# A hybrid DeltaNet layer on one Trainium2 core: delta values turned by VectorE over DRAM, the queries' sums of squares by VectorE and a small transfer

## The chip, the core and the metric

The kernel runs on one core of a Trainium2 chip. The core has TensorE (PE, with its weight loads PEld), VectorE (DVE), ScalarE (ACT), GpSimd (POOL) and SyncE (SP), each with its own queue of instructions that it takes in order; transfers are issued by an engine and then run on the core's 16 DMA engines. The metric is the device time of one execution in microseconds, as the median of several. The profile is of one execution.

## The reference

Two layers of a decoder trunk over 256 tokens with 1024 channels, batch 1, all in f32. A layer is a SwiGLU half step, a layer norm, three token mixers side by side on one combined input projection (gated DeltaNet, sliding-window attention, attention to a memory), gates, a projection of each mixer and of their gated sum, a layer norm, another SwiGLU half step and a layer norm. The change is in the DeltaNet mixer, of 4 heads with 128 channels:

```python
qkv = silu(causal_depthwise_conv(concat([q, k, v]), conv_w))
q = q * rsqrt(sum(q * q, -1) + 1e-6)            # per token and head
k = k * rsqrt(sum(k * k, -1) + 1e-6)
o = gated_delta_rule(q, k, v, g, beta)          # chunks, a triangular inverse each
o = o * rsqrt(mean(o * o, -1) + 1e-6) * norm_w
o = o * silu(z)
```

The kernel does not scale q and k themselves. It carries the keys' norms `kn` into the values (`vin` = v times kn, by token), and the queries' sums of squares into the epsilon of the last norm (`qeps` = 128e-6 times (sum of q squared + 1e-6)).

## The kernel before

Tokens come in two blocks of 128. All weights pass through one stream of units of 128 x 1024 f32. SP loads a unit into `raw` (4 buffers); ACT casts it to `whi`, DVE subtracts to `wlo` (`split`, L125; 5 buffers each), and PE multiplies it in three passes (every matmul is recorded at L134, the helper). A unit is released for the next when PE has used it. The stream runs ahead of PE by these buffers, and ACT and DVE take its casts and splits between all other work, in one fixed order for each engine that a scheduler made. PE's own order in the mixers is as written (`pinned`).

`conv` projects k, q and v channel by channel with tokens along the free axis (`kT`, `qT`, `vT`). What is needed with tokens on partitions is turned by PE: `tok` puts four 128x128 transposes (L137) into one PSUM bank. `tok_k` (during q's projection) and `tok_q` (during v's) take the sums of squares from there with a square on ACT and a reduction on DVE; `tok_v` (during the projection of the memory queries) multiplies the turned values by `kn` into `vin`.

Behind this, gates and branch projections are woven with small steps: `weave` runs a step's functions after the n-th yield of the projection, about 12 matmuls each. `inverses` (L783) sends the diagonal blocks over DRAM to POOL, which inverts them; `begin_inverse` (L902) hands them to DVE; seven calls of `double` join blocks on PE, with copies on ACT, DVE (L852, L853) and POOL (L878). Then `rec_v0` reads `vin` of block 0 on PE, `rec_s1` builds the state, `rec_r1` forms R1 on DVE (L945) from `vin` of block 1, and `rec_v1` reads R1 on PE. `finish` (L917) reads `qeps`. `branch(1)` holds its four units until its last group of matmuls; DVE multiplies each group by its gate (L998), and POOL adds it to the sum (L1000).

The FFN already turns its hidden activations without PE: `out` (L347) transposes 32x32 blocks on DVE (L356), writes them with four DMAs to DRAM (L362) and reads them back with one (L363), both issued by POOL.

Of the kernel before, what the change touches and what calls it, by code (L numbers as in the profile page):

```python
# [14 lines left out]
ALU = mybir.AluOpType  # L15
# [23 lines left out]
def tile_trunk(ctx, tc, x, xT, mem, memT_, wst, lnp, memln, cvw, rows, cst, out):  # L39
# [22 lines left out]
    def T(pool, shape, tag, dt=F32, bufs=None):  # L62
        pool = pn if pool is pu and tag in NEAR else pool
        kw = {} if bufs is None else {"bufs": bufs}
        return pool.tile(shape, dt, tag=tag, name=nm(tag), **kw)
# [79 lines left out]
    def weave(work, steps):  # L145

        for n, _ in enumerate(work, 1):
            for f in steps.get(n, ()):
                f()
# [374 lines left out]
    def mixers(l, hT, mkT, mv_, post):  # L524
# [35 lines left out]
        ktok = T(pu, [P, 4, P], "u9")  # L560
        vin = T(pu, [P, 2, 4, P], "u2")
        rk2 = T(pu, [P, 2, 4], "rk2")
# [24 lines left out]

        def tok_v():
            for tb in range(2):
                ps = tok(vT, tb)  # L590
                nc.vector.tensor_tensor(vin[:, tb], ps, kn[:, tb, :].unsqueeze(2).to_broadcast([P, 4, P]), op=ALU.mult)

        def tok_q():
            for tb in range(2):
                sumsq(tok(qT, tb), ssq[:, 1, tb, :])
            nc.vector.tensor_scalar(qeps, ssq[:, 1], RMS_EPS, RMS_EPS * P, ALU.add, ALU.mult)

        weave(conv(1, kT), {})
        weave(conv(0, qT), {3: [tok_k]})
        weave(conv(2, vT), {3: [tok_q]})  # L600

# [166 lines left out]
        def w_values(tb):  # L768
            if not oS:
                oS.extend(T(pu, [P, 4, S], tag, F32R) for tag in ("u6", "u7"))  # L770
            ts = slice(tb * P, (tb + 1) * P)
            pso = at()
            for kb in range(tb + 1):
                for kv in range(2):
                    hs = slice(kv * 64, kv * 64 + 64)
                    matmul(pso[hs, :], swv[:, kb, hs], wpT[tb][kb][:, kv].rearrange("p h q -> p (h q)"), start=kb == 0, stop=kb == tb)
            split(oS[0][:, :, ts], oS[1][:, :, ts], pso.rearrange("p (h k) -> p h k", h=4))

# [44 lines left out]

        weave(halves(xt, use_xq), {3: [tok_v]})
        (b,) = projB(xt, 1, 8)
# [12 lines left out]
        def doubling(c):  # L838
# [13 lines left out]
            nc.vector.tensor_tensor(Y32[:, c], Y32[:, c], ps, op=ALU.subtract)  # L852
            nc.vector.transpose(W[:, 512 + c * P:512 + c * P + P], W[:, 768 + c * P:768 + c * P + P])  # L853
            yield
# [22 lines left out]
            for q in qd:  # L877
                nc.gpsimd.tensor_copy(Yc[q, :, q], Y32[q, c])  # L878
            yield
# [56 lines left out]
        def rec_v0():  # L936
            nc.scalar.copy(V0, heads(lambda h: (Y[:, 0, h, :], vin[:, 0, h, :])))

# [3 lines left out]
        def rec_r1():  # L942
            ps = heads(lambda h: (kT[:, h, c1], S1[:, h, :]))
            for h in range(4):
                nc.vector.scalar_tensor_tensor(R1[:, h, :], ps[:, h, :], neg1[:, h:h + 1], vin[:, 1, h, :], op0=ALU.mult, op1=ALU.add)  # L945

# [38 lines left out]
        def branch(n, o):  # L985
# [4 lines left out]
            for tb in range(2):  # L990
                ts = slice(tb * P, (tb + 1) * P)
                for j in range(2):
# [4 lines left out]
                    dst = gt[tb] if n else mg[tb]  # L997
                    nc.vector.scalar_tensor_tensor(dst[:, js], gt[tb][:, js], 1.0, ps, op0=ALU.add, op1=ALU.mult)  # L998
                    if n:
# [17 lines left out]
            2: [lambda: w_scores(1, 1)],  # L1017
            3: [double],
            5: [double, lambda: w_turn(1, 0)],
            6: [double, lambda: w_turn(1, 1)],  # L1020
            7: [double, lambda: w_values(1)],
            8: [double]})
        weave(branch(1, oS), {
            1: [double],
            2: [rec_v0],
            3: [rec_s1],
            4: [rec_r1]})
# [176 lines left out]
```

## Time and profile before

| what | before |
|---|---|
| median of 3 runs | 1274.08 us (1273.45 to 1274.12) |
| profiled execution, span from the first to the last instruction | 1272.1 us |
| PE busy | 1260.6 us, 99% |
| DVE / ACT / POOL busy | 864.1 / 661.4 / 207.2 us |
| mean granted TensorE clock | 0.998 |

The profiled execution's own time is its span of 1272.1 us; the median of the runs is 1.98 us more, for what lies around the first and the last instruction. In a timeline a row gives start and duration in us, then engine, line of the kernel, operation, the tile written and the tiles read, and in brackets how long the engine was idle just before and on whom it waited. In the groups of instructions the figures behind the bar are busy us, mean ns of one, and idle us before. The chain of waits follows the work that ended last back from the end.

### The profile page before, as it was taken

Reading aid. Unit: us, or ns where it says so; the run is one execution under the profiler, and the core shown is the slowest. Engines: PE = TensorE matmul, PEld = TensorE weight load, DVE = VectorE, ACT = ScalarE, POOL = GpSimd, SP = SyncE. Lnnn points to the kernel's source line nnn. Section 1 sums busy time; section 2 is a strip of 40 time slices with the busy share of each in tenths; the row PEclk is TensorE's granted clock in tenths of the full one; section 3 lists DMA queues with packets and bytes.
Section 4 is the critical chain, followed back from the end, with each engine's and each line's share of the span. In section 5 each row is a group of like instructions: output and inputs, shape, how many; then the busy total and the mean of one; then the engine's idle time right before and its main releaser. Section 6 shows DMA issues by size and latency. Waiting matters only on the chain.

```text
span 1272.1 us, 18768 instructions
## 1 busy us (share of the span) xinstructions
PE 1260.6 (99%) x6948; PEld 1073.3 (84%) x6948; DVE 864.1 (68%) x1274; ACT 661.4 (52%) x982; POOL 207.2 (16%) x365
## 2 busy tenths in 40 slices
PE   9999999999999999999999999999999999999997
PEld 6888889999778888888888888899987788888886
DVE  6678576886647776665766665759867387766565
ACT  6456444655664544454454554456556554454441
POOL 1232000002311102221012220000023101122100
PEclk9999999999999999999999999999999999999999
DMA  8988765655534748877668877566463356577762
GB/s 294 317 271 289 248 208 159 211 171 129 172 117 144 241 141 259 241 241 220 217 210 244 256 252 219 177 185 213 150 167 134 100 189 225 174 246 244 241 220 82
DMA packets 77643, 261.40 MB, mean 205 GB/s; under 512 B 11920, under 2 KB 13328, under 8 KB 77552
## 3 DMA queue, kind: packets, MB, share of 16 engines
q1 hardware_dynamic: 66320, 232.40, 56.0%
q0 software_dynamic: 11088, 27.68, 8.1%
q8 instruction: 54, 0.88, 0.3%
q14 instruction: 37, 0.30, 0.1%
q10 hardware_dynamic: 144, 0.13, 0.0%
HBM read 246.40 MB, written 13.76 MB: 205 GB/s over the span
## 4 chain that ended last, share of the span: by engine, by line
PE 89%; DMA 3%; POOL 3%; DVE 2%; issue 2%; ACT 0%; SPq 0%; DVEq 0%; POOLq 0%; ACTq 0%
PE acc L134 80%; PE at L134 3%; PE sm L134 2%; DMA w<-dr 2%; PE sm L137 2%; DVE wlo L125 1%; DMA raw<-in_wst_dram 1%; POOL t L808 1%; POOL t L807 1%; PE acc L332 1%; PE acc L333 1%; POOL l L798 1%; PE acc L335 1%; DMA dr<-t 1%; ACT whi L125 0%
## 5 line engine op out<-in xcount | busy, mean ns | idle before, releaser
L125 DVE TENSOR_TENSOR wlo<-raw,whi 128x1024 fp32r<-128x1024 f32 (+2 forms) x405 | 487.0, 1210 | 279.7 <-ACT whi L125 277.5
L125 ACT CAST whi<-raw 128x1024 fp32r<-128x1024 f32 (+2 forms) x405 | 413.7, 1029 | 400.6 <-PE acc L134 316.2
L134 PE MATMUL acc<-whi,hT 128*128 128x512 f32 (+1 forms) x1824 | 562.2, 386 | 0.5 <-ACT whi L125 0.5
L134 PEld LDWEIGHTS acc<-whi,hT 128*128 128x128 f32 x1824 | 340.0, 188 | 69.8 <-ACT whi L125 2.3
L134 PE MATMUL acc<-wlo,hT 128*128 128x512 f32 (+1 forms) x912 | 350.2, 384 | 0.0
L134 PE MATMUL acc<-whi,u 128*128 128x512 f32 x812 | 259.5, 392 | 0.0
L134 PEld LDWEIGHTS acc<-wlo,hT 128*128 128x128 f32 x912 | 171.3, 188 | 33.1 <-DVE wlo L125 1.0
L134 PEld LDWEIGHTS acc<-whi,u 128*128 128x128 f32 x812 | 152.3, 188 | 32.1 <-DVE u L125 0.5
L134 PE MATMUL acc<-wlo,u 128*128 128x512 f32 x406 | 158.2, 390 | 0.0
L362 POOL DMA_DIRECT2D tr<-t x176 | 96.3, 554 | 311.6 <-DVE t L356 303.5
L134 PE MATMUL acc<-hT,whi 128*128 128x256 f32 x672 | 122.2, 284 | 0.0
L134 PEld LDWEIGHTS acc<-hT,whi 128*128 128x128 f32 x672 | 104.6, 192 | 0.0
L134 PE MATMUL acc<-hT,wlo 128*128 128x256 f32 x336 | 95.0, 283 | 0.0
L134 PEld LDWEIGHTS acc<-wlo,u 128*128 128x128 f32 x406 | 76.3, 188 | 15.4
L134 PEld LDWEIGHTS acc<-hT,wlo 128*128 128x128 f32 x336 | 64.3, 191 | 0.0
L363 POOL DMA_DIRECT2D pt<-tr x44 | 25.0, 569 | 192.5 <-DMA tr<-t 138.4
L353 ACT ACTIVATE t<-acc 128x256 f32<-128x256 f32 x88 | 33.5, 381 | 36.9 <-PE acc L134 36.9
L134 PE MATMUL acc<-u,u 128*128 128x512 f32 x186 | 46.4, 394 | 0.0
L354 DVE TENSOR_TENSOR t<-t,acc 128x256 f32<-128x256 f32 x88 | 36.6, 417 | 8.1 <-ACT t L353 4.1
L1000 POOL TENSOR_TENSOR u<-u,gt 128x512 f32<-128x512 f32 x16 | 20.7, 1294 | 125.0 <-DVE gt L998 125.0
L134 PEld LDWEIGHTS acc<-u,u 128*128 128x128 f32 x186 | 34.6, 188 | 7.5
L125 DVE TENSOR_TENSOR u<-pt,u 128x512 fp32r<-128x512 f32 x44 | 28.9, 657 | 9.4 <-ACT u L125 9.4
(236 smaller groups left out, 1165.0 us busy)
## 6 DMA issues: line engine op xcount, KB each, us to landing
raw<-in_wst_dram SPq DMA_DIRECT2D x409, 512.0 KB, 4.4
tr<-t POOLq DMA_DIRECT2D x176, 64.0 KB, 3.8
pt<-tr POOLq DMA_DIRECT2D x44, 256.0 KB, 5.0
raw<-in_wst_dram SPq DMA_DIRECT2D x16, 324.0 KB, 3.0
gB<-in_lnp_dram SPq DMA_DIRECT2D x6, 512.0 KB, 5.8
bB<-in_lnp_dram SPq DMA_DIRECT2D x6, 512.0 KB, 6.2
w<-dr POOLq DMA_DIRECT2D x4, 512.0 KB, 12.0
t<-in_xT_dram SPq DMA_DIRECT2D x4, 256.0 KB, 5.2
```

The lines of the kernel that those rows point to most:

```text
L125: return nc.scalar.copy(hi, src).ins, nc.vector.tensor_tensor(lo, src, hi.bitcast(F32), op=ALU.subtract).ins
L134: return pe(nc.tensor.matmul(*a, **k))
L137: return pe(nc.tensor.transpose(*a))
L332: nc.tensor.matmul(ps, hT[0][:, k, ts], hi[:, c], start=k == 0, stop=False)
L333: nc.tensor.matmul(ps, hT[0][:, k, ts], lo[:, c], start=False, stop=False)
L335: nc.tensor.matmul(ps, hT[1][:, k, ts], hi[:, c], start=False, stop=k == KD - 1)
L353: act = nc.scalar.activation(t[:, :, tb, :], g, AF.Silu).ins
L354: ins = nc.vector.tensor_tensor(t[:, :, tb, :], t[:, :, tb, :], u, op=ALU.mult).ins
L362: nc.gpsimd.dma_start(d[:, :, q].rearrange("b c x -> c b x"), z[32 * q:32 * q + 32].rearrange("c (b x) -> c b x", b=4))
L363: back = nc.gpsimd.dma_start(y, d.rearrange("b c q x -> (b c) (q x)")).ins
L798: nc.gpsimd.tensor_tensor(L32[q, c], AK[c][q, :, 0, q], cs[q, C_LV:C_LV + 32].unsqueeze(1).to_broadcast([32, 4, 32]), op=ALU.mult)
L1000: nc.gpsimd.tensor_tensor(mg[tb][:, js], mg[tb][:, js], gt[tb][:, js], op=ALU.add)
```

## The change

q's and v's transposes leave PE. `tok_q` and `tok_v` are gone; in their place stand five functions, in the doubling's steps (`gates(1)` and `branch(1)`).

- `leave_v` (step 3 of `gates(1)`): for each token block DVE turns 32x32 blocks of `vT` into a tile `z`, and POOL writes it with four DMAs to DRAM (`tv`, 64 KB each).
- `back_v` (step 5): for each block one DMA on POOL reads it back into `vin`, whose layout is now channel group, head, channel (256 KB each).
- `land_v` (step 7): DVE scales `vin` in place by `kn`, once a block.
- `leave_q` (step 8): for each block ACT squares `qT`, DVE turns the squares and reduces groups of 32 columns to `part`; one DMA on POOL writes all of `part` (128x32, 16 KB) to DRAM, and four read it back (4 KB each, in pieces of 32 bytes) with tokens on partitions.
- `land_q` (step 3 of `branch(1)`): DVE adds the four parts and forms `qeps`.

`held` puts each of these behind the instruction last noted in `late` on the same engine; this orders the queues and adds no wait of its own. `rec_v0` and `rec_r1` read `vin` in its new layout.

```diff
-        def tok_v():
-            for tb in range(2):
-                ps = tok(vT, tb)
-                nc.vector.tensor_tensor(vin[:, tb], ps, kn[:, tb, :].unsqueeze(2).to_broadcast([P, 4, P]), op=ALU.mult)
-
-        def tok_q():
+        def squares(src, tb):
+            return src[:, :, tb * P:(tb + 1) * P].rearrange("p h (q j) -> p q h j", q=4)
+
+        def leave_v():
             for tb in range(2):
-                sumsq(tok(qT, tb), ssq[:, 1, tb, :])
+                z = T(p2, [P, 512], "t2", bufs=4)
+                nc.vector.transpose(z, squares(vT, tb))
+                d = T(pd, [4, 32, 4, P], "tv")
+                for a in range(4):
+                    nc.gpsimd.dma_start(d[:, :, a].rearrange("t j x -> j t x"), z[32 * a:32 * a + 32].rearrange("j (t x) -> j t x", t=4))
+                turned_v.append(d)
+
+        def back_v():
+            for tb in range(2):
+                nc.gpsimd.dma_start(vin[:, tb].rearrange("p a h i -> p (a h i)"), turned_v[tb].rearrange("t j a x -> (t j) (a x)"))
+
+        def land_v():
+            for tb in range(2):
+                late["dve"] = nc.vector.tensor_tensor(vin[:, tb], vin[:, tb], kn[:, tb, :].unsqueeze(1).unsqueeze(3).to_broadcast([P, 4, 4, 32]), op=ALU.mult).ins
+
+        def leave_q():
+            part = T(p2, [P, 4, 8], "oqs")
+            for tb in range(2):
+                sq = T(p2, [P, 512], "t2", bufs=4)
+                nc.scalar.activation(sq.rearrange("p (q h j) -> p q h j", q=4, h=4), squares(qT, tb), AF.Square)
+                z = T(p2, [P, 512], "t2", bufs=4)
+                nc.vector.transpose(z, sq)
+                nc.vector.tensor_reduce(part[:, :, tb * 4:tb * 4 + 4], z.rearrange("p (q h i) -> p q h i", q=4, h=4), axis=AX.X, op=ALU.add)
+            d = T(pd, [4, 32, 4, 8], "tq")
+            nc.gpsimd.dma_start(d.rearrange("a j t x -> (a j) t x"), part)
+            sums_q.append(T(p2, [P, 4, 8], "oqr"))
+            for t in range(4):
+                nc.gpsimd.dma_start(sums_q[0][32 * t:32 * t + 32], d[:, :, t].rearrange("a j x -> j a x"))
+
+        def land_q():
+            nc.vector.tensor_reduce(ssq[:, 1].rearrange("p t h -> p (t h)"), sums_q[0].rearrange("p a x -> p x a"), axis=AX.X, op=ALU.add)
             nc.vector.tensor_scalar(qeps, ssq[:, 1], RMS_EPS, RMS_EPS * P, ALU.add, ALU.mult)
...
-        weave(conv(2, vT), {3: [tok_q]})
+        weave(conv(2, vT), {})
...
-        weave(halves(xt, use_xq), {3: [tok_v]})
+        weave(halves(xt, use_xq), {})
...
-            3: [double],
-            5: [double, lambda: w_turn(1, 0)],
+            3: [double, lambda: held(leave_v)],
+            5: [double, lambda: w_turn(1, 0), lambda: held(back_v)],
             6: [double, lambda: w_turn(1, 1)],
-            7: [double, lambda: w_values(1)],
-            8: [double]})
+            7: [double, lambda: w_values(1), lambda: held(land_v)],
+            8: [double, lambda: held(leave_q)]})
         weave(branch(1, oS), {
             1: [double],
             2: [rec_v0],
-            3: [rec_s1],
+            3: [rec_s1, lambda: held(land_q)],
             4: [rec_r1]})
```

The order of the queues at three places, all in layer 0 (layer 1 has the same). The lines of the changed kernel are higher by 38 from here on.

First DVE behind v's convolution, where `g` is formed, on which `decay`'s matmul waits (`spp` are the steps of a softplus, `u` a split of the memory queries, `swk` the window's keys). Before:

```order
L633 SCALAR_TENSOR_TENSOR spp_2575<-spp_2575,spz_456_2573 128x8
L125 TENSOR_TENSOR u_466_2597<-acc_2666,u_465_2596 128x512
L634 SCALAR_TENSOR_TENSOR spp_2575<-spp_2575,spz_2569 128x8
L635 TENSOR_SCALAR spp_2575<-spp_2575 128x8
L636 SCALAR_TENSOR_TENSOR spp_2575<-spt_2564,spp_2575 128x8
L638 TENSOR_TENSOR g_2586<-spp_2575,nea 128x8
L125 TENSOR_TENSOR wlo_2974<-raw_2972,whi_2973 128x1024
L125 TENSOR_TENSOR swk_100<-acc_2741,swk_99 64x256 x2
```

And now:

```order
L671 SCALAR_TENSOR_TENSOR spp_2558<-spp_2558,spz_452_2556 128x8 x3
L672 SCALAR_TENSOR_TENSOR spp_2558<-spp_2558,spz_2552 128x8
L673 TENSOR_SCALAR spp_2558<-spp_2558 128x8
L674 SCALAR_TENSOR_TENSOR spp_2558<-spt_2547,spp_2558 128x8
L125 TENSOR_TENSOR wlo_2945<-raw_2943,whi_2944 128x1024
L676 TENSOR_TENSOR g_2569<-spp_2558,nea 128x8
L125 TENSOR_TENSOR swk_100<-acc_2712,swk_99 64x256 x2
```

`g` now stands behind the split that it stood ahead of.

Then POOL from the end of the inverse on (`w` are the doubling's tiles, `u` with `tv` is `vin`, `u` with `gt` the merged sum). Before:

```order
L809 TENSOR_TENSOR w_470_2601<-t_535_3053,cs 128x256
L878 COPY w_471_2602<-w_470_2601 32x4x32 x8
L1000 TENSOR_TENSOR u_592_3349<-u_592_3349,gt_3450 128x512 x2
L1000 TENSOR_TENSOR u_593_3350<-u_593_3350,gt_3451 128x512 x2
L1000 TENSOR_TENSOR u_592_3349<-u_592_3349,gt_3944 128x512 x2
```

And now:

```order
L847 TENSOR_TENSOR w_466_2584<-t_529_3024,cs 128x256
L916 COPY w_467_2585<-w_466_2584 32x4x32 x8
L605 DMA tv_3591<-t_627_3589 32x4x128 x4
L605 DMA tv_3598<-t_629_3596 32x4x128 x4
L610 DMA u_390_2079<-tv_3591 128x512
L610 DMA u_390_2079<-tv_3598 128x512
L627 DMA tq_3827<-oqs_3816 128x32
L1038 TENSOR_TENSOR u_586_3320<-u_586_3320,gt_3421 128x512
L630 DMA oqr_3829<-tq_3827 32x4x8 x4
L1038 TENSOR_TENSOR u_586_3320<-u_586_3320,gt_3421 128x512
L1038 TENSOR_TENSOR u_587_3321<-u_587_3321,gt_3422 128x512 x2
```

The four ways back of the sums stand behind the first product of the branch, and the other three products behind them.

Last DVE from the split of the window's output (`u` of `at`) to R1 (`w` of `sm`). Before:

```order
L125 TENSOR_TENSOR u_615_3473<-at_3788,u_614_3472 128x4x128
L125 TENSOR_TENSOR wlo_3950<-raw_3948,whi_3949 128x1024
L998 SCALAR_TENSOR_TENSOR gt_3450<-gt_3450,acc_3851 128x512
L998 SCALAR_TENSOR_TENSOR gt_3450<-gt_3450,acc_3878 128x512
L998 SCALAR_TENSOR_TENSOR gt_3451<-gt_3451,acc_3899 128x512
L125 TENSOR_TENSOR wlo_3996<-raw_3994,whi_3995 128x1024
L125 TENSOR_TENSOR wlo_4027<-raw_4025,whi_4026 128x1024
L125 TENSOR_TENSOR wlo_4072<-raw_4070,whi_4071 128x1024
L125 TENSOR_TENSOR wlo_4094<-raw_4092,whi_4093 128x1024
L998 SCALAR_TENSOR_TENSOR gt_3451<-gt_3451,acc_3920 128x512
L945 SCALAR_TENSOR_TENSOR w_462_2591<-sm_3935,neg_460_2589,u_390_2079 128x128 x2
```

And now, down to the first of the same four splits:

```order
L614 TENSOR_TENSOR u_390_2079<-u_390_2079,kn_2081 128x512 x2
L624 STREAM_TRANSPOSE t_665_3819<-t_664_3817 128x512
L624 STREAM_TRANSPOSE t_667_3824<-t_666_3822 128x512
L625 TENSOR_REDUCE oqs_3816<-t_665_3819 128x4x4
L125 TENSOR_TENSOR wlo_3959<-raw_3957,whi_3958 128x1024
L625 TENSOR_REDUCE oqs_3816<-t_667_3824 128x4x4
L1036 SCALAR_TENSOR_TENSOR gt_3421<-gt_3421,acc_3858 128x512
L1036 SCALAR_TENSOR_TENSOR gt_3421<-gt_3421,acc_3885 128x512
L1036 SCALAR_TENSOR_TENSOR gt_3422<-gt_3422,acc_3906 128x512
L633 TENSOR_REDUCE ssq_2077<-oqr_3829 128x8
L634 TENSOR_SCALAR qeps_2082<-ssq_2077 128x8
L125 TENSOR_TENSOR wlo_4005<-raw_4003,whi_4004 128x1024
```

The scaling of the values and the squares' reductions stand ahead of the first gate product, and the sums' reduction (L633), which reads what the four small DMAs bring, between the third gate product and the four splits; what follows them is in the order of before.

More of the change, by code (lines that the diff above doesn't have):

```diff
@@ L560, in mixers @@
         ktok = T(pu, [P, 4, P], "u9")
-        vin = T(pu, [P, 2, 4, P], "u2")
+        vin = T(pu, [P, 2, 4, 4, 32], "u2")
         rk2 = T(pu, [P, 2, 4], "rk2")
@@ L586, in tok_k, with held @@
             nc.vector.tensor_tensor(kn, ssq[:, 0], kn, op=ALU.mult)
-        def tok_v():
-            for tb in range(2):
-                ps = tok(vT, tb)
-                nc.vector.tensor_tensor(vin[:, tb], ps, kn[:, tb, :].unsqueeze(2).to_broadcast([P, 4, P]), op=ALU.mult)
-        def tok_q():
-            for tb in range(2):
-                sumsq(tok(qT, tb), ssq[:, 1, tb, :])
+        late = {}
+        def held(f):
+            with ExitStack() as st:
+                for b in late.values():
+                    st.enter_context(tc.issue_after(b))
+                f()
@@ new lines, in back_v @@
+        def back_v():
+            for tb in range(2):
+                nc.gpsimd.dma_start(vin[:, tb].rearrange("p a h i -> p (a h i)"), turned_v[tb].rearrange("t j a x -> (t j) (a x)"))
+        def land_v():
+            for tb in range(2):
+                late["dve"] = nc.vector.tensor_tensor(vin[:, tb], vin[:, tb], kn[:, tb, :].unsqueeze(1).unsqueeze(3).to_broadcast([P, 4, 4, 32]), op=ALU.mult).ins
+        turned_v, sums_q = [], []
+        def leave_q():
[11 more added lines that the diff above has]
+                nc.gpsimd.dma_start(sums_q[0][32 * t:32 * t + 32], d[:, :, t].rearrange("a j x -> j a x"))
@@ L776, in w_values @@
                     matmul(pso[hs, :], swv[:, kb, hs], wpT[tb][kb][:, kv].rearrange("p h q -> p (h q)"), start=kb == 0, stop=kb == tb)
-            split(oS[0][:, :, ts], oS[1][:, :, ts], pso.rearrange("p (h k) -> p h k", h=4))
+            late["act"], late["dve"] = split(oS[0][:, :, ts], oS[1][:, :, ts], pso.rearrange("p (h k) -> p h k", h=4))
         qd = [slice(32 * i, 32 * i + 32) for i in range(4)]
@@ L852, in doubling @@
             nc.vector.tensor_tensor(Y32[:, c], Y32[:, c], ps, op=ALU.subtract)
-            nc.vector.transpose(W[:, 512 + c * P:512 + c * P + P], W[:, 768 + c * P:768 + c * P + P])
+            late["dve"] = nc.vector.transpose(W[:, 512 + c * P:512 + c * P + P], W[:, 768 + c * P:768 + c * P + P]).ins
             yield
@@ L877, in doubling @@
             for q in qd:
-                nc.gpsimd.tensor_copy(Yc[q, :, q], Y32[q, c])
+                late["pool"] = nc.gpsimd.tensor_copy(Yc[q, :, q], Y32[q, c]).ins
             yield
@@ L936, in rec_v0 @@
         def rec_v0():
-            nc.scalar.copy(V0, heads(lambda h: (Y[:, 0, h, :], vin[:, 0, h, :])))
+            nc.scalar.copy(V0, heads(lambda h: (Y[:, 0, h, :], vin[:, 0, :, h, :])))
         def rec_s1():
@@ L944, in rec_r1 @@
             for h in range(4):
-                nc.vector.scalar_tensor_tensor(R1[:, h, :], ps[:, h, :], neg1[:, h:h + 1], vin[:, 1, h, :], op0=ALU.mult, op1=ALU.add)
+                nc.vector.scalar_tensor_tensor(*(t[:, h, :].rearrange("p (a i) -> p a i", a=4) for t in (R1, ps)), neg1[:, h:h + 1], vin[:, 1, :, h, :], op0=ALU.mult, op1=ALU.add)
         def rec_qs():
@@ L997, in branch @@
                     dst = gt[tb] if n else mg[tb]
-                    nc.vector.scalar_tensor_tensor(dst[:, js], gt[tb][:, js], 1.0, ps, op0=ALU.add, op1=ALU.mult)
+                    late["dve"] = nc.vector.scalar_tensor_tensor(dst[:, js], gt[tb][:, js], 1.0, ps, op0=ALU.add, op1=ALU.mult).ins
                     if n:
```

## The prediction

> **What bounds the kernel now.** I read the page's busy shares first, then the chain of waits in order of time, then the timelines of layer 0 around the edited lines. The columns of the chain are start, us, what.
>
> ```profile
> span 1272.1 us, 18768 instructions
> PE 1260.6 (99%) x6948; PEld 1073.3 (84%) x6948; DVE 864.1 (68%) x1274; ACT 661.4 (52%) x982; POOL 207.2 (16%) x365
> 258.43 0.87 PE sm L137 x8
> 270.81 0.87 PE sm L137 x8
> 900.74 0.87 PE sm L137 x8
> ```
>
> PE is busy for 1260.6 of 1272.1 us, so only what shortens PE's own queue, or makes PE wait, moves the end. The pieces are the eight transposes of q and the eight of v in each layer, four in all, of which the first two and the last are shown. They lie on the chain themselves, with PE work directly before and after, so no other engine ends last there. Whether the whole 0.87 us is PE time shows in the timeline (start, us, engine, line, operation); the last row is the group of such transposes (busy, mean ns):
>
> ```profile
> 258.15 0.28 PE L134 MATMUL acc<-hT,wlo 128*128 128x256 f32 x1
> 258.27 1.04 PE L137 MATMUL sm<-cs,u 128*128 128x128 f32 x8
> 259.06 0.48 PE L134 MATMUL acc<-hT,whi 128*128 128x256 f32 x2
> 259.38 0.28 PE L134 MATMUL acc<-hT,wlo 128*128 128x256 f32 x1
> L137 PE MATMUL sm<-cs,u 128*128 128x128 f32 x80 | 11.0, 272 | 0.0
> ```
>
> A matmul of this projection takes a slot of 0.12 us (258.15 to 258.27), so three slots, 0.36 us, would lie between the two wlo matmuls if nothing stood between. It is 259.38 - 258.15 = 1.23 us. The difference is 0.87 us, the chain's figure: each transpose is recorded with 272 ns but takes a slot of 0.109, since they overlap.
>
> **What the change removes.** PE loses 4 x 8 transposes, 4 x 0.87 = **3.48 us**, and gets nothing in return: its order differs in no other row. DVE and ACT lose work in the same place (over both layers four squares, four reductions and four scalings by the keys' norms), which only helps there.
>
> One thing behind v moves against PE. g, on which the decay matmul waits, is now queued on DVE behind one more weight split.
>
> ```profile
> 277.35 1.05 ACT L125 CAST whi<-raw 128x1024 fp32r<-128x1024 f32 x1 [1.35 <-PE acc L134]
> 278.18 0.17 DVE L638 TENSOR_TENSOR g<-spp,nea 128x8 f32<-128x8 f32 x1
> 278.43 1.23 DVE L125 TENSOR_TENSOR wlo<-raw,whi 128x1024 fp32r<-128x1024 f32 x1
> 280.15 0.51 PE L134 MATMUL sm<-g,cs 128*128 128x8 f32 x4
> ```
>
> All of this moves with PE, so I keep the old clock: the split ends at 279.66, g at 279.8, and PE wants it at 280.15. It costs nothing, with 0.3 us to spare.
>
> **What it adds, and where.** Everything new stands between 357 and 389 us of the old clock (and 629 us later in layer 1), on DVE, ACT, POOL and POOL's DMAs. The rows that price it are groups (busy, mean ns), issues with KB and median us to landing, and the span of landings of the FFN's turn:
>
> ```profile
> L356 DVE STREAM_TRANSPOSE t<-t 128x512 f32<-128x512 f32 x44 | 31.3, 711 | 1.3
> L575 DVE TENSOR_REDUCE ssq<-t 128x4 f32<-128x512 f32 x8 | 5.4, 676 | 0.0
> L591 DVE TENSOR_TENSOR u<-sm,kn 128x512 f32<-128x512 f32 x4 | 2.7, 688 | 1.1 <-PE sm L137 1.1
> L362 POOL DMA_DIRECT2D tr<-t x176: 548/551/712, 21.2 to 1212.4; - x176
> DMA to landing us min/median/max: 2.0/3.8/6.0
> pt<-tr POOLq DMA_DIRECT2D x44, 256.0 KB, 5.0
> dr<-t POOLq DMA_DIRECT2D x2, 64.0 KB, 3.3
> ms<-mst POOLq DMA_DIRECT2D x4, 0.5 KB, 4.4
> ```
>
> The rows of DVE and POOL between which it falls, and the last wait of PE behind it:
>
> ```profile
> 356.60 0.31 DVE L853 STREAM_TRANSPOSE w<-w 128x128 f32<-128x128 f32 x1
> 356.63 1.27 POOL L878 COPY w<-w 32x128 f32<-32x128 f32 x4 [0.54 <-DVE w L852]
> 371.96 0.69 DVE L125 TENSOR_TENSOR u<-at,u 128x512 fp32r<-128x512 f32 x1 [0.81 <-ACT u L125]
> 375.35 1.23 DVE L125 TENSOR_TENSOR wlo<-raw,whi 128x1024 fp32r<-128x1024 f32 x1 [2.70 <-ACT whi L125]
> 378.29 0.69 DVE L998 SCALAR_TENSOR_TENSOR gt<-gt,acc 128x512 f32<-128x512 f32 x1 [1.72 <-PE acc L134]
> 379.13 1.28 POOL L1000 TENSOR_TENSOR u<-u,gt 128x512 f32<-128x512 f32 x1 [21.23 <-DVE gt L998]
> 382.12 1.05 PE L134 MATMUL sm<-u,w 128*128 128x128 f32 x8
> 385.95 0.69 DVE L998 SCALAR_TENSOR_TENSOR gt<-gt,acc 128x512 f32<-128x512 f32 x1 [2.94 <-PE acc L134]
> 388.62 4.63 DVE L125 TENSOR_TENSOR wlo<-raw,whi 128x1024 fp32r<-128x1024 f32 x4 [1.98 <-ACT whi L125]
> 389.87 3.66 DMA raw<-in_wst_dram
> 394.71 1.59 DVE L125 TENSOR_TENSOR wlo<-raw,whi 128x1024 fp32r<-128x1024 f32 x1 [0.34 <-ACT whi L125]
> 396.22 0.59 DVE L945 SCALAR_TENSOR_TENSOR w<-sm,neg,u 128x128 f32<-128x128 f32 x2
> 396.97 1.13 PE L134 MATMUL sm<-w,w 128*128 128x128 f32 x8 [0.16 <-DVE w L945]
> ```
>
> Values, out and back. Two transposes of 0.71 us follow L853, until 358.3. They are hidden in DVE's waits. POOL is free at 357.9; eight issues of 0.55 us put the last at 361.8, landed at 365.6 (3.8), the second way back issued some 0.5 us later and landed at 371.1 (5.0). DVE comes to the scaling at 372.65, so it does not wait. With the slowest of the FFN's turns (6.0) it would be 373.3, 0.6 late. The first reader on PE starts at 382.12, so the values themselves have 8 us of cover after the scaling (to 374.0).
>
> The queries' squares. Two transposes and two reductions after 374.0 (2 x 0.71 + 2 x 0.68) with the old split of 1.23 us among them end at about 378.0; less the overlap of some 0.08 us that successive DVE rows show, 377.6. Nothing of PE hangs on it: the next gt at 378.29 is hardly touched. The two squares on ACT fit in gaps before 374.1.
>
> The sums' way. POOL issues the way out at 377.6. The tile is small (16 KB) and no row has its form; the nearest are 3.3 us (64 KB), 4.4 us (0.5 KB, in a busier stretch) and the FFN's 2.0 to 6.0. The queue is empty here:
>
> ```profile
> 380.00:384.00 4.00, 4.00 (x23) 3.42 (x23) 0.69 (x1) 0.59 (x1) 1.33 (x2) 1.00 0.01 3
> ```
>
> (the last two figures: DMA share 0.01, 3 GB/s). I take 3.3 us, landed 380.9. POOL has done its product at 380.4, waits 0.5 us more for the issue, and its four small ways back start at 381.4 to 383.0; the last lands at 386.3. DVE has done its third gt at 386.6, sums the 32 columns and forms qeps in about 0.4 us, and is ready at 387.0. **Behind it on DVE** stand four weight splits, which start at 388.62 because ACT does, and behind these R1 (L945), for which PE already waits 0.16 us. So the new wait has 1.6 us of cover. If it is used up, PE pays one for one: the first of the splits frees the buffer of the raw transfer (3.66 us), whose split stands directly ahead of R1's second half.
>
> Bounds: with 2.0 us each way DVE is not held at all; with 6.0 us each way the sums are there at 377.6 + 6.0 + 0.5 + 1.65 + 6.0 + 0.4 = 392.1, 3.5 us late, in each layer. The edge is (388.6 - 377.6 - 0.5 - 1.65 - 0.4) / 2 = 4.2 us a way; the gain of 1.74 us a layer is gone at 5.1 us.
>
> The Trainium skill, "DMA: Bandwidth & Descriptors", section "Anatomy of one DMA", puts a DMA from GpSimd at about 2.0 us plus bytes / 436e3. By that the sums would be ready at about 384 us, and the term is nothing too. Its section "Specifications" says that transfers of under 512 B lose line rate because they are read, modified and written, which speaks against the four ways back with their 32 B pieces; no issue of this trace has such pieces, so nothing here tells whether it holds.
>
> **Sum.** 1272.1 - 3.48 = 1268.6 us of span. The median before is 1274.08, 1.98 above the profiled span; the same offset gives **1270.6 us**.
>
> **Rivals.**
> 1. The inverse chain does not come with PE. Between 294 and 342 us the chain of waits runs over POOL and a DMA, DVE stands 4.5 us for it, and PE idles.
>
> ```profile
> 310.58 12.10 DMA w<-dr
> 337.24 0.45 DVE L902 STREAM_TRANSPOSE w<-w 128x256 f32<-128x256 f32 x1 [4.52 <-POOL w L809]
> 342.86 1.08 PE L134 MATMUL at<-pt,swv 128*64 128x512 f32 x4 [0.61 <-DVE pp L741]
> 940.43 11.71 DMA w<-dr
> ```
>
> If that DMA met other traffic because all is 1.74 us earlier, each us more is a us of PE in that layer. Against it: the chain starts from PE's products and shifts with them, and the two layers differ by 0.39 us only. Half a us to a whole one lost in each layer: 1271.6 to 1272.6.
> 2. The sums come back late, between the edge and the break-even (4.2 to 5.1 us a way): 0 to 1.74 us a layer given back, 1270.6 to 1274.1, mostly within no change.
> 3. The other side: one mechanism, the same wait of DVE at the sums (L633), beyond 5.1 us a way. At 6.0 it costs 2 x 3.5 = 7.0 us against 3.48: 1277.6, slower. For it: small pieces and four issues in a row; against it: an empty DMA queue and the 3.3 us of dr<-t in a fuller one.
> 4. A transpose costs PE its recorded duration, not its slot. The Trainium skill, "TensorE: Matmul & The Clock Gate", section "Part 4: PE-mode transpose", gives about 275 ns in a kernel's context. If they did not overlap, 32 x 0.272 = 8.7 us of PE would go, and the time would be 1265.4. Against it: the row of eight lasts 1.04 us, and the next matmul starts 0.79 us after its start.
>
> **Chances.** The forecast 0.62, with its own range 1270.0 to 1271.5; rival 1 0.13; rival 2 0.14; rival 3 0.09; rival 4 0.02. Faster or slower counts from 0.2%, about what this kernel's measurement tells from no change: below 1271.5 and above 1276.6. Faster: 0.62 + 0.02 and 0.03 of rivals 1 and 2 = 0.67. Slower: most of rival 3 and a tail of others, 0.09. Same: the rest, 0.24. The range of 8 in 10 takes the forecast, rival 1 and the better part of rival 2: **1269.8 to 1273.6**.
>
> **What would show it.** Right: 6916 PE rows, no L137 piece of eight at about 258 and 270 us; the matmuls of rec_v1 near 395.2 us with an idle of some 0.2 us before; on DVE the scaling (L614) starts right behind the split before it, and L633 is over before ACT has cast for the next split. Wrong: DVE idle before L633 with a DMA as its releaser and more than 0.5 us of PE idle before the matmuls of rec_v1; or more than 0.6 us of PE idle at w_values near 341 us; or the landings of the sums' DMAs above 4.2 us. The price of a transpose is wrong if all these waits are as before and the time still isn't 3.5 us lower.

## The result and the profile after

| what | before | after |
|---|---|---|
| median of 13 runs each, side by side | 1274.55 us | 1271.33 us (1270.30 to 1274.34) |
| ratio | 1 | 0.9978, 95% interval 0.9971 to 0.9985 |
| span of the profiled execution | 1272.1 us | 1270.1 us |
| PE busy, matmul records | 1260.6 us, 6948 | 1258.1 us, 6916 |
| DVE / POOL busy | 864.1 / 207.2 us | 871.3 / 221.0 us |

The kernel is 3.2 us faster by these medians, and 2.8 us by the ratio; 1270.6 us was predicted, within 1269.8 to 1273.6. The page of the changed kernel (engines: busy us, share, instructions) and its group of such transposes (busy us, mean ns):

```profile
span 1270.1 us, 18774 instructions
PE 1258.1 (99%) x6916; PEld 1070.9 (84%) x6916; DVE 871.3 (69%) x1284; ACT 661.5 (52%) x982; POOL 221.0 (17%) x395
L137 PE MATMUL sm<-cs,u 128*128 128x128 f32 x48 | 6.9, 272 | 0.0
```

32 records are gone from the group of 80, at the same 272 ns each. PE's busy time fell by 2.5 us though, not by 32 x 0.272 = 8.7 us. DVE and POOL do 7 and 14 us more, and PE does not wait for it.

To see where the span went I cut each profile at the same PE rows in both layers: the start of the keys' transposes, the first matmul of the scores, the first matmul of rec_v1 and one and the same matmul of the next FFN. Two such rows of PE's timeline (start, us, engine, line, operation; the count at the end is of the shown window, which ends before the eighth transpose), before,

```profile
245.89 0.93 PE L137 MATMUL sm<-cs,u 128*128 128x128 f32 x7
284.27 0.60 PE L134 MATMUL at<-u,u 128*128 128x256 f32 x3
```

and after:

```profile
246.10 0.60 PE L137 MATMUL sm<-cs,u 128*128 128x128 f32 x4
282.83 0.37 PE L134 MATMUL at<-u,u 128*128 128x256 f32 x1
```

The first stretch is the one that held the transposes: 284.27 - 245.89 = 38.38 us, now 282.83 - 246.10 = 36.73. All stretches of the two profiles:

| stretch | before | after | difference |
|---|---|---|---|
| start to the keys' transposes, layer 0 | 245.89 | 246.10 | +0.21 |
| keys' transposes to scores | 38.38 | 36.73 | -1.65 |
| scores to rec_v1 (all new work is here) | 112.70 | 112.22 | -0.48 |
| rec_v1 to the next FFN | 68.27 | 68.87 | +0.60 |
| FFN to the keys' transposes, layer 1 | 410.57 | 410.68 | +0.11 |
| keys' transposes to scores | 38.39 | 36.73 | -1.66 |
| scores to rec_v1 | 112.22 | 113.08 | +0.86 |
| rec_v1 to the next FFN, and to the end | 245.68 | 245.69 | +0.01 |

The two stretches of the removal give 3.31 us. The other rows, +0.21, -0.48, +0.60, +0.11, +0.86 and +0.01, add up to +1.31; 3.31 - 1.31 = 2.0 us of span. The question for the experiments is whether these other differences belong to the change.

The new work in layer 0 of the changed kernel, timelines of DVE and POOL. First the values:

```profile
354.92 1.26 DVE L602 STREAM_TRANSPOSE t<-u 128x512 f32<-128x512 f32 x2
355.93 4.44 POOL L605 DMA_DIRECT2D tv<-t  x8
362.29 0.57 POOL L610 DMA_DIRECT2D u<-tv  x1 [1.91 <-DMA tv<-t]
364.04 0.56 POOL L610 DMA_DIRECT2D u<-tv  x1 [1.18 <-DMA tv<-t]
370.65 1.28 DVE L614 TENSOR_TENSOR u<-u,kn 128x512 f32<-128x512 f32 x2
```

The scaling (L614) has no bracket: it starts right behind the split before it, and the values have long landed. Then the sums:

```profile
374.76 0.68 DVE L625 TENSOR_REDUCE oqs<-t 128x16 f32<-128x512 f32 x1
375.73 0.54 POOL L627 DMA_DIRECT2D tq<-oqs  x1 [11.13 <-DVE oqs L625]
379.89 2.21 POOL L630 DMA_DIRECT2D oqr<-tq  x4 [1.40 <-DMA tq<-oqs]
384.03 0.69 DVE L1036 SCALAR_TENSOR_TENSOR gt<-gt,acc 128x512 f32<-128x512 f32 x1 [2.94 <-PE acc L134]
384.63 0.20 DVE L633 TENSOR_REDUCE ssq<-oqr 128x8 f32<-128x32 f32 x1
384.86 1.30 POOL L1038 TENSOR_TENSOR u<-u,gt 128x512 f32<-128x512 f32 x1 [1.43 <-DVE ssq L633]
384.87 1.32 DVE L634 TENSOR_SCALAR qeps<-ssq 128x8 f32<-128x8 f32 x1
386.70 4.63 DVE L125 TENSOR_TENSOR wlo<-raw,whi 128x1024 fp32r<-128x1024 f32 x4 [0.51 <-ACT whi L125]
394.31 0.59 DVE L983 SCALAR_TENSOR_TENSOR w<-sm,neg,u 128x128 f32<-128x128 f32 x2
395.05 1.13 PE L134 MATMUL sm<-w,w 128*128 128x128 f32 x8 [0.15 <-DVE w L983]
```

L633 did not wait for its DMA either, the splits still start when ACT is ready, and rec_v1 idles for 0.15 us, where it was 0.16. One row is a surprise: the step that forms `qeps` on 8 columns takes 1.32 us. It starts with POOL's product of 1.30 us and ends 0.03 us behind it. Of the 1.98 us that DVE had idle ahead of the splits, 0.51 are left.

The new transfers (KB each, median us from issue to landing), layer 0:

```profile
tv<-t POOLq DMA_DIRECT2D x8, 64.0 KB, 3.8
u<-tv POOLq DMA_DIRECT2D x2, 256.0 KB, 3.2
oqr<-tq POOLq DMA_DIRECT2D x4, 4.0 KB, 1.8
tq<-oqs POOLq DMA_DIRECT2D x1, 16.0 KB, 3.9
```

### The profile page after: what moved, and what is told of

Read it like the earlier page. It is cut to its first block, busy times and chain, and to the rows that moved or that the text cites. A ratio compares the mean times of both kernels' runs of the same rounds, so it can differ in the third digit from the quotient of the medians.

```text
span 1270.1 us, 18774 instructions
## 1 busy us (share of the span) xinstructions
PE 1258.1 (99%) x6916; PEld 1070.9 (84%) x6916; DVE 871.3 (69%) x1284; ACT 661.5 (52%) x982; POOL 221.0 (17%) x395
## 4 chain that ended last, share of the span: by engine, by line
PE 94%; DVE 3%; DMA 2%; ACT 1%; issue 1%; SPq 0%; DVEq 0%; ACTq 0%
PE acc L134 83%; PE at L134 3%; PE sm L134 3%; DMA raw<-in_wst_dram 2%; PE sm L137 1%; DVE wlo L125 1%; PE acc L335 1%; PE acc L332 1%; PE at L137 1%; PE acc L333 1%; ACT whi L125 1%; DVE h L291 0%; DVE h L296 0%; DVE h L418 0%; DVE bnst L277 0%
## 5 line engine op out<-in xcount | busy, mean ns | idle before, releaser
L134 PEld LDWEIGHTS acc<-whi,hT 128*128 128x128 f32 x1824 | 340.5, 188 | 68.9 <-issue 1.6
L553 DVE SCALAR_TENSOR_TENSOR t<-acc,cw,t 128x255 f32<-128x255 f32 (+2 forms) x72 | 34.5, 479 | 1.1
```

What stands on the lines that cost most here:

```text
L134: return pe(nc.tensor.matmul(*a, **k))
L553: nc.vector.scalar_tensor_tensor(yc[:, j, d:], b[:, j, :S - d], w[:, t:t + 1], yc[:, j, d:], op0=ALU.mult, op1=ALU.add)
```

## The experiments

Theory: the gain is PE's 32 slots and nothing else, the new work is covered, and the differences in the other stretches come and go with the execution. Rivals: the new work costs some of the gain, by the sums' wait or by what it does to the inverse's transfers; or removing the transposes itself makes something late.

**The removal without the new work, and the change again.** In the first the DMAs, the turns and the sums are left out, and all that reads the values and the sums computes on constants:

```diff
+        nc.gpsimd.memset(vin, 0.01)
+        nc.gpsimd.memset(qeps, 0.01)
...
-            3: [double, lambda: held(leave_v)],
-            5: [double, lambda: w_turn(1, 0), lambda: held(back_v)],
+            3: [double],
+            5: [double, lambda: w_turn(1, 0)],
...
-            7: [double, lambda: w_values(1), lambda: held(land_v)],
-            8: [double, lambda: held(leave_q)]})
+            7: [double, lambda: w_values(1)],
+            8: [double]})
...
-            3: [rec_s1, lambda: held(land_q)],
+            3: [rec_s1],
```

> The changed kernel without any of the new work: q's and v's transposes are gone from PE, and nothing turns them elsewhere; the values and the queries' sums are left out and filled with constants by POOL at the layer's start, so all behind them computes on constants. PE's order is that of the changed kernel. Theory of slots (4 pieces of 0.87 us of PE, the late work covered): 3.48 us under before, ratio 0.9973, and the same time as the changed kernel within 0.5 us; PE arrives 1.66 to 1.74 us earlier in each layer at the first matmuls behind the convolutions. Rival (the late work on DVE, ACT and POOL costs PE what the profile of the change lacks, 2.0 us instead of 3.48): 0.7 to 1.5 us faster than the changed kernel in the same runs. Rival (transposes cost PE their recorded 272 ns): 8.7 us under before.

> The changed kernel once more, beside the others on one chip, for a second profile. Theory of slots: 3.48 us under before, ratio 0.9973. In the profile, between the landmarks (k's transposes, the first matmuls of the scores, the first doubling, rec_v1, the next FFN) the convolutions give 1.7 us a layer as in the first profile, while the other differences of the first pair (+0.4 and -0.9 us at the inverse chain, -0.6 us at the layer norm behind the mixers) come out otherwise, since they are landings of transfers. Rival (the change itself costs 0.6 to 0.9 us at these places): the same differences again.

**One piece alone.** In the one kernel `tok_v` is kept as it was and the queries go the new way; in the other `tok_q` is kept and the values go the new way:

```diff
-        weave(halves(xt, use_xq), {})
+        weave(halves(xt, use_xq), {3: [tok_v]})
```

```diff
-        weave(conv(2, vT), {})
+        weave(conv(2, vT), {3: [tok_q]})
```

> Only the queries' part: squares turned by DVE and sent over DRAM, v's transposes stay on PE. Theory of slots: half of the gain, 1.74 us under before, ratio 0.9986, and no wait of DVE before the sums' reduction. Rival (the sums' way costs PE): less than 1.74, and v alone gets the larger part.

> Only the values' part: v turned by DVE over DRAM, q's transposes and sums of squares stay as before. Theory of slots: half of the gain, 1.74 us under before, ratio 0.9986. Rival (the 1 MB each layer that the values move over DRAM delays raw transfers or the inverse): less than 1.74, and q alone gets the larger part.

**The kernel before, again.**

> The kernel before once more, for a second profile of it. If the segments of the first profile are its own: 38.4 us from the key transposes to the scores in each layer, 112.2 to 112.7 from the scores to the value product of chunk 1, 68.3 from there to the next feed-forward in both layers, with no idle TensorE at the layer norm behind the mixers. If the 0.6 to 1.5 us that layer 0 lost there in three profiles without the eight transposes of either piece is nothing but chance, it may show here too (over 69).

Measured (the first four share their runs of the kernel before, median 1274.53; the last ran beside 1274.37):

| kernel | median us | ratio, 95% interval | span |
|---|---|---|---|
| removal alone | 1271.03 | 0.9975 (0.9966 to 0.9983) | 1270.2 |
| change again | 1271.31 | 0.9974 (0.9964 to 0.9983) | 1270.3 |
| queries alone | 1272.50 | 0.9984 (0.9975 to 0.9994) | 1270.7 |
| values alone | 1272.73 | 0.9985 (0.9976 to 0.9993) | 1271.2 |
| before again | 1274.33 | 1.0003 (0.9994 to 1.0012) | 1272.1 |

And the stretches of their profiles, with a third one of the change (below); layer 0 / layer 1:

| kernel | start | keys to scores | scores to rec_v1 | rec_v1 to FFN |
|---|---|---|---|---|
| before | 245.89 | 38.38 / 38.39 | 112.70 / 112.22 | 68.27 / 68.29 |
| before again | 245.98 | 38.38 / 38.39 | 112.23 / 112.21 | 68.28 / 68.64 |
| queries alone | 246.56 | 37.53 / 37.52 | 112.24 / 112.22 | 68.30 / 68.32 |
| values alone | 246.41 | 37.59 / 37.59 | 112.25 / 112.65 | 68.30 / 68.27 |
| removal alone | 246.26 | 36.74 / 36.73 | 112.22 / 112.23 | 69.74 / 68.28 |
| change | 246.10 | 36.73 / 36.73 | 112.22 / 113.08 | 68.87 / 68.28 |
| change again | 246.54 | 36.74 / 36.74 | 112.26 / 112.25 | 69.53 / 68.29 |
| change, third | 246.84 | 36.73 / 36.75 | 112.22 / 112.23 | 68.28 / 68.27 |

Read by columns this settles where the gain comes from. The queries' piece is worth 0.85 to 0.87 us, the values' 0.79 to 0.80, both 1.64 to 1.66, to 0.02 us in every profile. The column with all the new work reads 112.2 with it and without it, so the late work costs nothing to 0.04 us where the inverse is in time. (The 112.65 of the values alone is a wait of 0.54 us at rec_v1 in one layer, which no other of these profiles has.) Its two larger values in the first pair of profiles (112.70 before, 113.08 after) come once in each of the two kernels, so nothing ties them to the change. There the inverse's chain was late, as these rows of the changed kernel's layer 1 show (DVE's and PE's timeline, then POOL's transfer):

```profile
964.73 0.45 DVE L940 STREAM_TRANSPOSE w<-w 128x256 f32<-128x256 f32 x1 [4.93 <-POOL w L847]
970.34 1.08 PE L134 MATMUL at<-pt,swv 128*64 128x512 f32 x4 [1.04 <-DVE pp L779]
w<-dr POOLq DMA_DIRECT2D x2, 512.0 KB, 12.9
```

In the kernel before the same transfer took 11.8 us in layer 1, and PE idled for 0.18. In the two layers of the 13 profiles of this study PE idled here four times for over 0.3 us, once in the kernel before and once in the change.

The first column differs by up to 0.95 us ahead of the transposes that are gone. It was lowest in the two profiles of the kernel before, which is part of why the spans show less than the medians.

**A loss in layer 0 that is in three of these profiles.** The last column reads 68.3, but 68.9, 69.5 and 69.7 in three profiles of kernels without either piece, one of which has no new work at all. The rival "the removal makes something late" has its place here. In the chain of waits of the changed kernel a weight unit takes 6.15 us, and PE then waits for the layer norm:

```profile
431.79 6.15 DMA raw<-in_wst_dram
437.96 1.06 ACT whi L125
```

PE's and ACT's timelines of the same kernel show both ends:

```profile
436.68 1.05 ACT L125 CAST whi<-raw 128x1024 fp32r<-128x1024 f32 x1 [1.39 <-DMA raw<-in_wst_dram]
456.20 1.29 PE L137 MATMUL sm<-cs,h 128*128 128x128 f32 x8 [0.41 <-DVE h L296]
```

The unit stands in SP's queue behind two loads of 512 KB, the layer norm's gain and bias (`gB`, `bB`), at 427.12 and 427.96 us. Between 424 and 426 us the DMA engines moved nothing. So I moved the loads ahead of the last weight unit of the gated sum's projection, by a call of a new function of `Post` that makes them once:

```diff
+        def ready(self):
+            if self.gb is None:
+                self.gb = gb(*self.aps)
...
-                self.gb = gb(*self.aps)
+                self.ready()
...
+            if (tb, uu) == (0, 1):
+                post.ready()
             if len(wo) < KD:
                 fetch()
```

> The change with the two 512 KB loads of the layer norm's gain and bias issued one weight unit earlier on SP, at about 418.7 us of layer 0 instead of 427, where the DMA engines are idle. Theory (the 0.6 to 1.5 us that layer 0 lost in three profiles is a weight unit that lands late behind these two loads): the casts of ScalarE at 434 to 441 wait less than 0.6 us each, TensorE has no idle time at the layer norm, 68.3 us from the value product of chunk 1 to the feed-forward in both layers, and the median is 0.3 to 1.2 us under the change's: 1270.0 to 1271.0, ratio 0.9965 to 0.9973. Rival (the transfers are slow at that time whatever stands beside them): a cast there waits over 2 us for its unit again and the median is the change's, 0.9974 to 0.9978.

> The loads of gain and bias one weight unit earlier, a second time beside the change. Theory (the two loads stand in the way of the unit): no cast at 432 to 441 us waits over 1.2 us, TensorE has no idle time at the layer norm, 68.3 us to the feed-forward in both layers, median 0.2 to 0.8 us below the change's in this call. Rival (no difference): the medians agree within 0.2 us.

> The change once more, beside the same kernel with the two loads moved. Theory (whether a weight unit lands late behind the loads of gain and bias is chance of the single execution, in the profiles so far 3 of 4 where TensorE came to the layer norm of layer 0 before 425 us): median 1271.0 to 1271.6, ratio 0.9972 to 0.9979; in the profile either 68.3 us from the value product of chunk 1 to the feed-forward of layer 0, or 68.9 to 69.7 with a cast that waits 1.4 us or more for its unit. Rival (the loss is gone with the next chip or run): 68.3.

Measured: 1271.03 us, ratio 0.9970 (0.9960 to 0.9980); again 1270.77, 0.9962 (0.9950 to 0.9974), beside the change's third with 1271.40, 0.9971 (0.9961 to 0.9981), and a kernel before of 1275.97 there. The loads now start at 418.6 us (SP's timeline of the kernel with the loads moved). The DMA engines are not idle then, as the expectation has it: in the changed kernel they are 99% busy from 418 to 420 us. But the loads have landed by 426.3 us, and so use the idle time from 424 on. No cast of layer 0 waits for more than 1 us, where less than 0.6 was expected (ACT's, the longest wait):

```profile
418.62 0.43 SPq L78 DMA_DIRECT2D gB<-in_lnp_dram  x1
419.10 0.42 SPq L78 DMA_DIRECT2D bB<-in_lnp_dram  x1
439.72 1.05 ACT L125 CAST whi<-raw 128x1024 fp32r<-128x1024 f32 x1 [0.99 <-DMA raw<-in_wst_dram]
```

rec_v1 to the FFN is 68.3 us in both profiles and layers. But the change's third profile has 68.28 too, with the loads where they were. And the kernel before has such a loss in its second profile, in layer 1 (the 68.64 of the table). Its ACT and PE there:

```profile
1072.23 1.05 ACT L125 CAST whi<-raw 128x1024 fp32r<-128x1024 f32 x1 [1.81 <-DMA raw<-in_wst_dram]
1087.01 1.29 PE L137 MATMUL sm<-cs,h 128*128 128x128 f32 x8 [0.38 <-DVE h L296]
```

So a loss of this kind, if a smaller one (0.36 us), does not need the removal. In layer 0 it fell in three of six profiles without both pieces, in none of three with the loads moved (the third follows), and in none of the four others. The three are the ones of those ten profiles with the loads unmoved in which the loads were issued earliest: at 427.12 to 427.60 us, the others from 427.86 on. This speaks for the earlier time as a part of the cause, and then some of the removal's gain would be lost there; ten executions do not show it. Over all runs of the three change kernels and of the three with moved loads the medians are 1271.35 (30 runs) and 1271.02 (19 runs), 0.33 us apart, with a 95% interval, by drawing the runs anew, of -0.02 to 0.91. That moving the loads helps is likely, and not shown. Why the unit lands late in some executions stays open: in the three profiles with the loss the two loads took 7.0 to 8.1 us, in the others without moved loads 5.3 to 6.6, though nothing new runs at that time.

**The sums made late.** To price the wait at the sums, two more transfers from DRAM to DRAM were put in their way, and the splits of units 1 to 3 of the last gates were queued behind `qeps` on DVE:

```diff
+            for n in range(2):
+                e = T(pd, [4, 32, 4, 8], f"tq{n}")
+                nc.gpsimd.dma_start(e.rearrange("a j t x -> (a j) (t x)"), d.rearrange("a j t x -> (a j) (t x)"))
+                d = e
...
-            nc.vector.tensor_scalar(qeps, ssq[:, 1], RMS_EPS, RMS_EPS * P, ALU.add, ALU.mult)
+            late["sums"] = nc.vector.tensor_scalar(qeps, ssq[:, 1], RMS_EPS, RMS_EPS * P, ALU.add, ALU.mult).ins
...
-                    hi, lo = unit()
+                    hi, lo = unit(behind=late["sums"] if n == 2 and 2 * j + uu in (1, 2, 3) else None)
```

> The change with the queries' sums sent through two further buffers in DRAM, and the splits of the last gates queued on VectorE behind the sums. Theory (there is a cover of some 0.5 us before the four splits that TensorE waits for, and beyond it every us of lateness counts once per layer): two hops of 2.9 to 3.9 us, less the 0.3 us between the landings and the reduction, make qeps ready at 390 to 392 instead of 386.2, the first split is over at 391.2 to 393.1 where TensorE needs it at 388.6, so 2.7 to 4.7 us per layer, 5.4 to 9.4 in all against the change: 1276.7 to 1280.7, a ratio to the kernel before of 1.0017 to 1.0049. Rival (the sums are off the path however late, since only the chunk's norm at 395.5 reads them and TensorE has other work): 1271 to 1272, ratio 0.997 to 0.998.

Measured: 1272.89 us, ratio 0.9985 (0.9976 to 0.9994): 1.56 us over the change, far less than the 5.4 to 9.4 expected, and more than the rival's nothing. In the profile each layer loses 0.5 us between the scores and rec_v1 (112.73 and 112.76). Layer 1 loses another 0.56 between rec_v1 and the FFN (68.84), where ACT stands for 3.79 us at a weight unit, at 1043.93; whether the late sums brought that about is not shown. DVE, POOL and PE of this kernel in layer 0, where all stands 0.72 us later than in the change's profile (283.55 against 282.83 at the scores):

```profile
388.45 0.69 DVE L1040 SCALAR_TENSOR_TENSOR gt<-gt,acc 128x512 f32<-128x512 f32 x1 [3.01 <-PE acc L134]
389.09 0.22 DVE L637 TENSOR_REDUCE ssq<-oqr 128x8 f32<-128x32 f32 x1
389.22 1.31 POOL L1042 TENSOR_TENSOR u<-u,gt 128x512 f32<-128x512 f32 x1 [0.28 <-DVE gt L1040]
389.31 0.40 PE L134 MATMUL acc<-wlo,hT 128*128 128x512 f32 x1
389.35 1.22 DVE L638 TENSOR_SCALAR qeps<-ssq 128x8 f32<-128x8 f32 x1
390.48 4.62 DVE L125 TENSOR_TENSOR wlo<-raw,whi 128x1024 fp32r<-128x1024 f32 x4
395.02 1.11 DVE L987 SCALAR_TENSOR_TENSOR w<-sm,neg,u 128x128 f32<-128x128 f32 x4
396.28 1.13 PE L134 MATMUL sm<-w,w 128*128 128x128 f32 x8 [0.66 <-DVE w L987]
```

The expectation failed in two terms. The hops took 2.0 us each by this kernel's transfers, not 2.9 to 3.9. And PE does not need the first of the four splits at 388.6: it multiplies a `wlo` with `hT` at 389.31, without a wait, when none of them has begun. What it needs from DVE is R1, behind them. On the change's clock the splits start at 390.48 - 0.72 = 389.76, which is 3.06 us later than 386.70. R1 is over at 396.13 - 0.72 = 395.41, only 0.51 later than 394.90, and PE's wait has grown by the same 0.51 (0.66 - 0.15). The other 2.55 us were given back by the order of this kernel: the fourth gate product (0.69) now stands ahead of the wait, and the split that stood inside R1 in the change (1.7) now follows it. So PE pays one for one for a later end of R1, but the cover is what stands between the wait and R1, and a scheduler that moves two rows changes it by 2.5 us.

**The reduction placed later.** The reduction and the step that makes `qeps` go one group later, where POOL has no product in hand:

```diff
-            3: [rec_s1, lambda: held(land_q)],
+            3: [rec_s1],
...
-            1: [rec_o0],
+            1: [lambda: held(land_q), rec_o0],
```

> The change with the reduction of the sums and the step that makes qeps placed one group later, behind the transposed norms of chunk 1, where GpSimd has no product in hand. Theory (the 1.32 us of the 8-column step come from GpSimd's product of 1.30 us beside it, and cost cover alone): the step takes 0.15 to 0.25 us, the four splits start about 1.5 us after the third gate sum or when ScalarE's cast is ready, and the time is the change's to 0.5 us, ratio 0.9970 to 0.9980. Rival (the step is slow because its input has just landed by DMA, or because of its shape in that place): 1.0 us or more there too.

Measured: 1271.33 us, 0.9975 (0.9965 to 0.9985), the change's time. DVE in layer 0:

```profile
387.71 4.63 DVE L125 TENSOR_TENSOR wlo<-raw,whi 128x1024 fp32r<-128x1024 f32 x4 [1.98 <-ACT whi L125]
395.84 0.19 DVE L633 TENSOR_REDUCE ssq<-oqr 128x8 f32<-128x32 f32 x1
396.55 0.15 DVE L634 TENSOR_SCALAR qeps<-ssq 128x8 f32<-128x8 f32 x1
```

The same step on the same operands takes 0.15 us without a product beside it, and DVE has its 1.98 us ahead of the splits again. So the 1.32 us come of POOL's product beside it, and they cost cover and no time.

**Both moves in one kernel.**

> Both moves in one kernel: the loads one weight unit earlier, and the sums' reduction behind the norms of chunk 1. Theory (the 1.32 us step costs cover alone and no time): the same as with the loads moved alone, within 0.3 us. Rival (the cover of 0.5 us is now and then not enough): lower by 0.3 us or more.

Measured: 1270.91 us, 0.9963 (0.9951 to 0.9975), 0.14 over the loads moved alone, side by side. The two are not told apart.

## Why the prediction was right, point by point

**What bounds the kernel: right.** What shortened PE's own queue moved the end. DVE and POOL got 21 us more between them and the time fell.

**The price of a transpose: right, rival 4 fell.** The queries' piece alone is 0.85 to 0.87 us, by the prediction's 0.87 for eight; at the recorded 272 ns it would be 2.2. This agrees with the row that the prediction took, and not with the figure of the Trainium skill, "TensorE: Matmul & The Clock Gate", section "Part 4: PE-mode transpose", of about 275 ns, as a price for a stream of them.

**g costs nothing: wrong by a tenth of a us.** The step that failed is "it costs nothing, with 0.3 us to spare". The values' piece gives 0.79, not 0.87. PE's row that waits for g, and DVE's with g:

```profile
278.32 0.16 DVE L676 TENSOR_TENSOR g<-spp,nea 128x8 f32<-128x8 f32 x1
278.63 0.57 PE L134 MATMUL sm<-g,cs 128*128 128x8 f32 x4
279.06 0.48 PE L134 MATMUL acc<-hT,whi 128*128 128x256 f32 x2
```

g ends 0.15 us ahead of its reader, and the four small matmuls take 279.06 - 278.63 = 0.43 us of PE, where they took 280.51 - 280.15 = 0.36 before. The queries-alone kernel is the test of the cause: it keeps v's transposes, and its DVE has g ahead of the split, in the old order (DVE's and PE's timelines):

```profile
278.00 0.17 DVE L681 TENSOR_TENSOR g<-spp,nea 128x8 f32<-128x8 f32 x1
279.97 0.51 PE L134 MATMUL sm<-g,cs 128*128 128x8 f32 x4
280.33 0.48 PE L134 MATMUL acc<-hT,whi 128*128 128x256 f32 x2
```

There g ends 1.80 us ahead of its reader, the four take 0.36 us again, and the piece is worth the full 0.87. In both layers of all 13 profiles they take 0.36 to 0.37 us where g ends 1.8 us ahead and 0.42 to 0.44 where it ends 0.15 ahead. So the later g goes with the loss, though no kernel differs in g's place alone.

**The values: right, with room.** The reads back landed in 3.2 us where 5.0 was taken, and the scaling had about 3 us of cover instead of 1.5. The landing of the last write was 3.8, as taken.

**The sums: right in what they cost, wrong in two sizes that nearly cancel.** The region runs 1.92 us earlier than in the profile before (386.70 for 388.62). On the old clock the way out was issued at 377.65, the ways back began at 381.8, and the sums were summed at 386.8: the prediction had 377.6, 381.4 and less than 387.0. The way out took 3.9 us (2.9 in layer 1) and the ways back 1.8, where 3.3 each was taken, all below the edge of 4.2 a way. The queries-alone kernel has it the other way round (layer 0):

```profile
oqr<-tq POOLq DMA_DIRECT2D x4, 4.0 KB, 3.3
tq<-oqs POOLq DMA_DIRECT2D x1, 16.0 KB, 1.8
```

What decides is the weight unit on SP's queue. In the change one was issued at 374.87 us, 0.86 ahead of the way out, and took 4.6; the way out landed 0.17 us behind it. In the queries-alone kernel the unit was issued at 375.97, behind the way out and 0.8 ahead of the ways back, and these landed 0.2 to 0.8 us behind it, the slowest after 3.85 us. So the prediction's "the queue is empty here" holds for the ways back alone: its window of 380 to 384 us begins 2.4 us behind the issue of the way out. That the sum of both ways still came out near the predicted one is in part luck. The pieces of 32 bytes did no harm that one can see where no unit was on its way. The failed term is "sums the 32 columns and forms qeps in about 0.4 us": it took 0.20 + 1.32. It left 0.5 us of cover for the predicted 1.6, and so the edge was nearer than the prediction thought, by 0.6 us a way if the step keeps this length. The clue stood in a quoted row of the kernel before: the split at 394.71 took 1.59 us instead of 1.2, and POOL had a product from 393.93 to 395.22.

**Rivals 2 and 3** did not occur. Their rule, that PE pays one for one once the cover is gone, is borne out by the 0.51 us that came of 0.51; their break-even is not, for it took the order behind the wait as given.

**Rival 1** came in part: in one of three profiles of the change the inverse's chain came 0.86 us late in layer 1. It came without the change too, in one of the two profiles of the kernel before, 0.48 us late in layer 0. So it does not need the change; whether the change makes it more frequent or longer, so few profiles do not tell.

**The sum.** 3.48 us was predicted and the two stretches give 3.31, the rest being g. By medians side by side it is 3.2 us; the kernel without the new work gives 3.5. The predicted 1268.6 us of span came out as 1270.1 because three stretches were longer in the one execution profiled (+0.21, +0.60, +0.86; +0.11 between the layers) and one shorter (-0.48). The 0.86 and the 0.48 are not repeated by the other profiles of the two kernels. The start was later than 245.89 in every other profile of the table too (by 0.1 to 0.95 us), and the 0.60 of the layer norm came again, larger, in two more profiles without both pieces. That its mean price is nothing is not shown; the prediction has no term for it.

## What to carry to other kernels

Price work that leaves a saturated engine by the slot between its neighbours in the timeline, not by its recorded duration: here the two differ by 2.5 times. Cover behind a wait must be read as the whole way to the next row that the bounding engine needs, row by row in its queue's order, and a tiny instruction in it can take the duration of what another engine does beside it. What a small transfer takes is read with the transfers that were issued just ahead of it: here the same one took 1.8 or 3.9 us. When a change is worth 0.25% and a span shows less, cut several profiles at the same rows: the stretches that hold the change agree to 0.02 us where spans differ by 1.

## What the runs showed of the hardware that was not expected

One small VectorE step can last as long as the GpSimd product beside it, and the small step ahead of it does not. The step that makes `qeps` (a TENSOR_SCALAR on 8 columns) took 1.32 and 1.31 us in the change's two layers, ending 0.03 us after products of 1.30 us. With the sums late it took 1.22 and 0.92, where the product had begun 0.13 and 0.41 us before it, and ended with it again; with no product beside it, 0.15. A gate product on DVE that reads PSUM kept its 0.69 us beside one (with the sums late, at 388.45; the product from 387.63 to 388.94). Two more rows of DVE bound the reading, the reduction with the sums late in layer 1 and the step with the loads moved in layer 0:

```profile
1017.79 0.23 DVE L637 TENSOR_REDUCE ssq<-oqr 128x8 f32<-128x32 f32 x1 [0.23 <-DMA oqr<-tq]
384.77 0.17 DVE L638 TENSOR_SCALAR qeps<-ssq 128x8 f32<-128x8 f32 x1
```

The reduction ran wholly beside a product (1017.64 to 1018.94) and took 0.23 us, against 0.20 with none. And the step took 0.17 us once although a product started with it, at 384.77; that product took 1.33 us instead of 1.30.

The Trainium skill, "SBUF — State Buffer", section "SBUF: two separate sides", states that VectorE and GpSimd share a port pair as an exclusive lock: whichever starts first holds it for its whole instruction and the other blocks. It states this of VectorE instructions in a two-port mode or with two SBUF inputs only. The long steps and the unhindered gate product and reduction agree with that, if the step that makes `qeps` runs in such a mode, which no row shows. In the one short case the step would have come first; the records put the two starts within 0.01 us in that case and in the change, so they do not tell who was first.

A small transfer on POOL's queue lands with the weight unit that was issued just ahead of it. The 16 KB from SBUF to DRAM took 1.8 us in the queries-alone kernel, with no unit on its way, and 2.9 to 3.9 in the others, landing 0.16 to 0.20 us behind a unit of 512 KB in both layers of all eight profiles that have both pieces. The four of 4 KB back in 32-byte pieces took 1.8 to 2.1 us in the change's three profiles and 2.0 to 3.9 in the queries-alone kernel, behind a unit. Two of 16 KB from DRAM to DRAM took about 2.0 each.
